# Block sums of feed-forward weights on GpSimd a group ahead, and token sums in place

## The chip, the cores and the metric

The kernel runs on one core of one Trainium2 chip. The metric is the device time of one execution in microseconds, lower is better: the median of several runs. TensorE does the matrix products, VectorE (DVE) and ScalarE (ACT) and GpSimd (POOL) the elementwise work, and SyncE (SP) issues the DMAs.

## The reference, cut to what matters

The reference is a two-layer decoder in float32: 512 tokens, width 1024, 16 heads, feed-forward width 2816. Layer 0 mixes tokens by stick-breaking attention, layer 1 by dilated attention. Each layer then does

```python
def _swiglu(h, w_gate, w_up, w_down):
    return (jax.nn.silu(h @ w_gate) * (h @ w_up)) @ w_down

h = h + _swiglu(_rmsnorm(h, norm_ffn[layer]), w_gate[layer], w_up[layer], w_down[layer])
```

The change touches only the two products `h @ w_gate` and `h @ w_up` of both layers.

## The kernel before, in words

Activations lie transposed: 1024 channels are 8 chunks of 128 partitions, with the 512 tokens along the free axis. A float32 product is made of three matmuls: every weight tile and every activation is split into a high part (fp32r, written by ACT, L306) and the remainder (a DVE subtraction, L307), and high x high, high x low and low x high are added in PSUM.

**The feed-forward.** The 2816 hidden channels are 22 chunks f of 128. Chunks 0 and 1 are computed plainly (`first_tiles`). Chunks 2 to 21 go in ten groups g of two chunks. For each chunk the gate and the up weights and the two halves of the channels form a 2x2 matrix of blocks, w00, w01 (gate) and w10, w11 (up), each 128x512; the tokens are halved too, and seven products P1 to P7 take the place of eight (a Strassen-Winograd scheme). Three products use raw blocks. Four use sums of blocks: S1 = w10 + w11, S2 = S1 + w00, S3 = w10 + w00, S4 = S2 + w01. The order in a group is P1, P2, P6 (S2), P5 (S1), P7 (S3), P4, P3 (S4), for both chunks each, 24 matmuls of 256 columns per product. Beside the products run the down projections (`down`) of earlier chunks, up to eight in a group, as `ffn_order` and `BESIDE` list them.

**Weights.** The class `Weights` is a stream. `load` has SP fetch blocks in their order of first use into two rings of eight slots (raw, raw2); a slot is free after the last product that uses its block. `split` makes one product's operand: where it is a sum, DVE adds first (L280, L281 for S1 and S2, into tiles called sum; L287 for S3, in place; L291 for S4, in place in the tile of S2), then ACT writes the high part and DVE the low part. `get` hands an operand to TensorE and calls `split` up to six operands ahead, as far as the rings allow. The 160 sums (20 chunks, four sums, two layers) are all DVE's before the change.

**Token sums.** Four of the seven products also need sums of token blocks. `token_sums` copies the normalised activations into B (128 x 8 x 512), makes four sums of 128x1024 on DVE (L919, L923, L927, L931) into two tiles tk, and splits each into XT (L913, L916). `first_tiles` lays these steps beside the matmuls of chunk 1.

**Elementwise work of a group.** After P2 DVE adds and scales the gate; after P7, P4 and P3 it adds the up parts (L1016, L1018, L1025). GpSimd multiplies each up tile by the row of scale factors (`scaled_up`, L968), and DVE multiplies gate and up (L971). GpSimd has little else to do here: L866 in `first_tiles`, which multiplies the gate of chunks 0 and 1, and later the gains of layer 1's weights (L305).

**Order.** Each engine works through its own queue in order. The framework inserts the semaphores and may place independent instructions of an engine otherwise than the source does: in the trace the four small column steps (L467 to L470) alternate with the token sums.

Of the kernel before, what the change touches and what calls it, by code (L numbers as in the profile page):

```python
# [7 lines left out]
F = mybir.dt.float32  # L8
# [71 lines left out]
def weight_stream():  # L80


    units, ops, place = [], [], {}

    def unit(key, width):
        if key not in place:
            place[key] = len(units)
            units.append((key, width))
        return place[key]

    for layer in range(2):
        for kind, i in mixer_order():
            r = (kind, layer, i)
            for j in range(4):
                gain = None
                if layer == 1 and kind == "qk":
                    which, part = (j % 2, j // 2) if crossed(r) else (j // 2, j % 2)
                    gain = ("k", (G_MIX1, G_KV)[which] + 4 * part)
                elif layer == 1 and kind == "v":
                    gain = ("v", G_KV + 2 * j)  # L100
                ops.append((kind, "mix", ("raw", unit((*r, j), 512)), gain))
        for step in ffn_order():
            if step[0] == "gu":
                for j in range(4):
                    ops.append(("gu", "mix", ("raw", unit(("gu", layer, step[1], j), 512)), None))
            elif step[0] == "dn":
                a, b = PARTS[step[1]]
                held = layer == 1 and step[1] == len(PARTS) - 1
                ops.append(("dn", "held" if held else "ffn",
                            ("raw", unit(("dn", layer, *step[1:]), 128 * (b - a))), None))  # L110
            else:
                for i in range(2):
                    f = 2 * step[1] + i
                    w = lambda r, c: unit(("w", layer, f, r, c), 512)
                    what = {"P1": lambda: ("raw", w(0, 0)), "P2": lambda: ("raw", w(0, 1)),
                            "P6": lambda: ("s2", w(1, 0), w(1, 1), w(0, 0)), "P5": lambda: ("s1",),
                            "P7": lambda: ("s3", w(1, 0), w(0, 0)), "P4": lambda: ("raw", w(1, 1)),
                            "P3": lambda: ("s4", w(0, 1))}[step[2]]()
                    ops.append(("pr", "ffn", (*what, i) if what[0][0] == "s" else what, None))
    return units, ops  # L120


# [67 lines left out]
class Weights:  # L190
# [8 lines left out]
    def __init__(self, tc, pool, wflat, gains):  # L199
        self.tc, self.nc, self.pool, self.w, self.gains = tc, tc.nc, pool, wflat, gains  # L200
        self.units, self.ops = weight_stream()
        self.offs = np.concatenate([[0], np.cumsum([128 * n for _, n in self.units])]).tolist()
        last = {}
        for n, op in enumerate(self.ops):
            for u in self.used(op):
                last[u] = n
        self.ends = {}
        for u, n in last.items():
            self.ends.setdefault(n, []).append(u)
        first = {}  # L210
# [18 lines left out]
        self.pools = {"raw": pool, "w": pool}  # L229
        self.rt, self.wt, self.sums = {}, {}, {}  # L230
        self.nload = self.nsplit = self.nget = 0

    @staticmethod
    def used(op):
        what = op[2]
        return {"raw": what[1:], "s2": what[1:4], "s1": (), "s3": what[1:3], "s4": what[1:2]}[what[0]]

    def load(self):
        u = self.nload
# [28 lines left out]
    def split(self):  # L268
# [6 lines left out]
        r = [self.rt[v] for v in self.used(self.ops[u])]  # L275
        if what[0] == "raw":
            v = r[0]
        elif what[0] == "s2":
            s1, s2 = (self.pools["sum"].tile([128, 512], F, name="sum", bufs=4) for _ in range(2))
            nc.vector.tensor_add(s1, r[0], r[1])  # L280
            nc.vector.tensor_add(s2, s1, r[2])  # L281
            self.sums[what[-1]] = (s1, s2)
            v = s2
        elif what[0] == "s1":
            v = self.sums[what[-1]][0]
        elif what[0] == "s3":
            nc.vector.tensor_add(r[0], r[0], r[1])  # L287
            v = r[0]
        else:
            v = self.sums.pop(what[-1])[1]  # L290
            nc.vector.tensor_add(v, v, r[0])  # L291
        n = v.shape[1]
        ring = self.oring[u]
        if ring == "held":
# [17 lines left out]
            self.live[self.uring[v]] -= 1  # L312
        self.nsplit += 1
        self.loads()

    def get(self, kind):
        u = self.nget
# [11 lines left out]
def trunk(ctx, tc, xg, wflat, cst_d, cs_d, outT):  # L329
# [510 lines left out]
    def ffn(layer, done):  # L840
# [36 lines left out]
        def first_tiles(p, XT):  # L877
# [3 lines left out]
            both("gu", banks)  # L881
            sums, columns, rows = rstd_steps(pjbank)
            sums()
            tau1, tau2, low1, low2, tau4, tau3, low4, low3 = token_sums(p, XT)
# [15 lines left out]

        def token_sums(p, XT):

            B = p.tile([128, 8, 512], F, name="B")
            t = [p.tile([128, 4, 256], F, name=f"tk{i}") for i in range(2)]
            b12, b21, b22 = B[:, 0:4, 256:512], B[:, 4:8, 0:256], B[:, 4:8, 256:512]
            b11 = B[:, 0:4, 0:256]

            def block(c):
                g = gains[:, (G_FFN0, G_FFN1)[layer] + c:(G_FFN0, G_FFN1)[layer] + c + 1]
                act.activation(B[:, c, :], H[:, c, :], AF.Copy, scale=g)  # L910

            def high(i, v):
                act.activation(XT[:, i, 0], v, AF.Copy)  # L913

            def low(i, v):
                dve.tensor_sub(XT[:, i, 1], v, XT[:, i, 0].bitcast(F))  # L916

            def first():
                dve.tensor_sub(t[0], b11, b12)  # L919
                high(1, t[0])  # L920

            def second():
                dve.scalar_tensor_tensor(t[1], t[0], -1.0, b22, op0=OP.mult, op1=OP.subtract)  # L923
                high(0, t[1])
# [11 lines left out]
            return [first, second, lambda: low(1, t[0]), lambda: low(0, t[1]), fourth, third,  # L936
                    lambda: low(3, t[0]), lambda: low(2, t[1])]

        st = {}

# [40 lines left out]
        def product(g, p, XT):  # L981
# [16 lines left out]
                    stepped()  # L998
            a, b, c, e = (st.get(k) for k in "abce")
            f0 = 2 * g  # L1000
            if p == "P1":
                st["g", 0] = TS()
                act.activation(st["g", 0], a, AF.Copy)
            elif p == "P2":
# [95 lines left out]
        order = ffn_order()  # L1100
        with tc.tile_pool(name=f"ff{layer}", bufs=1, reuse_waits="tile") as fp:
            XT = fp.tile([128, 4, 2, 4, 256], FR, name="XT")
            W.pools["w2"] = fp
            with tc.tile_pool(name=f"tk{layer}", bufs=1, reuse_waits="tile") as tp:
                first_tiles(tp, XT)
            with tc.tile_pool(name=f"wr{layer}", bufs=1, reuse_waits="tile") as wp:
                W.pools["raw2"] = W.pools["sum"] = wp
                W.loads()
                for step in order[2:]:
                    if step[0] == "pr":  # L1110
                        product(*step[1:], XT)
# [51 lines left out]
```

## Time and profile before

| what | value |
|---|---|
| median of 3 runs | 1210.62 us (1208.28 to 1211.24) |
| profiled execution: its own time, its span | 1206.98 us, 1205.1 us |
| mean granted TensorE clock | 0.997 |
| PE busy | 1185.0 us, 98% |
| DVE busy | 1011.8 us, 84% |
| ACT busy | 698.5 us, 58% |
| POOL busy | 173.8 us, 14% |
| DVE, low parts of weights (L307, four largest groups) | 206.8 + 71.0 + 45.6 + 37.4 us |
| DVE, block sums (L280, L281, L287, L291) | 160 instructions, mean 686 to 740 ns |
| POOL, `scaled_up` (L968) | 40 instructions, mean 1563 ns |

Busy is the time in which an engine executes an instruction; an instruction that is held up by something that the profile doesn't name counts as busy for longer. The matmuls are pipelined, so a busy PE is not a PE at its peak. The feed-forward of layer 0 with its sums runs from about 254 us to 610 us of the span, that of layer 1 from about 846 us to the end.

### The profile page before, as it was taken

The numbers are of one execution on the slowest core, as the hardware profiler recorded it, in microseconds if no ns is written. First come the engines' busy times: TensorE is split into PE (matmuls) and PEld (weight loads), VectorE is DVE, ScalarE is ACT, GpSimd is POOL, SyncE is SP. The second block draws the span as 40 slices with busy tenths as digits, with TensorE's granted clock in tenths as the row PEclk, the third lists the DMA queues.
The fourth block names the chain that finished last, engine by engine and source line by source line (L and its number), as shares of the span: only waits on it lengthen the run. The fifth ranks groups of instructions, "written<-read, shape, count | busy, mean of one in ns | idle before, by whom it ended". The sixth has DMA issues, their size and how long they took to land.

```text
span 1205.1 us, 21100 instructions
## 1 busy us (share of the span) xinstructions
PE 1185.0 (98%) x7501; PEld 1059.8 (88%) x7501; DVE 1011.8 (84%) x1831; ACT 698.5 (58%) x1331; POOL 173.8 (14%) x237
## 2 busy tenths in 40 slices
PE   9999999999999999999999999999999999999997
PEld 7989888888999999999788889887789999999996
DVE  6799999899987878787868899788899878787865
ACT  6667676685544444454466677767755444445443
POOL 0000000001100000014235443110111000000111
PEclk9999999999999999999999999999999999999998
DMA  7654644234243323332154656551343333333112
GB/s 265 177 147 113 159 114 124 62 105 140 88 125 95 115 88 114 98 106 88 36 142 132 158 136 178 133 149 53 96 141 124 113 100 102 98 113 89 45 61 70
DMA packets 74360, 138.30 MB, mean 115 GB/s; under 512 B 9616, under 2 KB 13712, under 8 KB 74256
## 3 DMA queue, kind: packets, MB, share of 16 engines
q1 hardware_dynamic: 74256, 136.97, 40.0%
q8 instruction: 59, 0.97, 0.3%
q14 instruction: 45, 0.37, 0.1%
HBM read 106.00 MB, written 2.10 MB: 90 GB/s over the span
## 4 chain that ended last, share of the span: by engine, by line
PE 87%; DVE 6%; issue 2%; DMA 2%; ACT 2%; SPq 1%; POOL 1%; POOLq 0%; DVEq 0%
PE pj L387 39%; PE z L387 30%; PE t L387 12%; PE av L387 3%; PE t L703 3%; DVE wlo L307 1%; DMA mov<-hl 1%; DMA raw<-wflat 1%; DVE w2lo L307 0%; DVE H L751 0%; SPq L243 0%; DMA H<-xg 0%; POOL H L1076 0%; DMA rp<-rp 0%; DVE sum L281 0%
## 5 line engine op out<-in xcount | busy, mean ns | idle before, releaser
L306 ACT ACTIVATE whi<-raw 128x512 fp32r<-128x512 f32 (+1 forms) x290 | 178.7, 622 | 134.5 <-PE pj L387 52.1
L307 DVE TENSOR_TENSOR wlo<-raw,whi 128x512 fp32r<-128x512 f32 (+1 forms) x290 | 206.8, 721 | 26.0 <-ACT whi L306 23.6
L387 PE MATMUL pj<-VO,whi 128*128 128x512 f32 x568 | 180.7, 398 | 1.1 <-DVE H L751 1.0
L387 PE MATMUL pj<-X,whi 128*128 128x512 f32 x480 | 154.4, 402 | 0.4
L968 POOL TENSOR_TENSOR up<-up,R 128x512 f32<-128x512 f32 x40 | 62.4, 1563 | 490.9 <-DVE up L1016 442.6
L387 PEld LDWEIGHTS pj<-VO,whi 128*128 128x128 f32 x568 | 102.4, 189 | 23.8 <-ACT whi L306 1.1
L387 PE MATMUL pj<-VO,wlo 128*128 128x512 f32 x284 | 112.7, 397 | 0.0
L751 DVE TENSOR_TENSOR H<-H,pj 128x512 f32<-128x512 f32 (+1 forms) x120 | 79.3, 664 | 32.2 <-PE pj L387 31.5
L387 PEld LDWEIGHTS pj<-X,whi 128*128 128x128 f32 x480 | 86.9, 188 | 19.1 <-ACT X L423 0.9
L387 PE MATMUL z<-XT,whi 128*128 128x256 f32 x560 | 99.7, 280 | 0.0
L306 ACT ACTIVATE w2hi<-raw 128x512 fp32r<-128x512 f32 (+1 forms) x102 | 62.8, 617 | 59.0 <-PE z L387 17.1
L387 PE MATMUL z<-X,whi 128*128 128x256 f32 (+1 forms) x464 | 96.1, 301 | 0.0
L387 PE MATMUL pj<-X,wlo 128*128 128x512 f32 x240 | 95.2, 396 | 0.5 <-DVE wlo L307 0.5
L387 PEld LDWEIGHTS z<-XT,whi 128*128 128x128 f32 x560 | 86.2, 189 | 0.7
L387 PE MATMUL pj<-VO,w2hi 128*128 128x512 f32 x264 | 83.1, 396 | 0.4 <-ACT VO L974 0.4
L307 DVE TENSOR_TENSOR w2lo<-raw,w2hi 128x512 fp32r<-128x512 f32 (+1 forms) x102 | 71.0, 698 | 12.0 <-ACT w2hi L306 11.7
L387 PEld LDWEIGHTS z<-X,whi 128*128 128x128 f32 x464 | 74.9, 189 | 4.7
L387 PE MATMUL z<-XT,wlo 128*128 128x256 f32 x280 | 78.5, 280 | 0.0
L387 PE MATMUL pj<-whi,X 128*128 128x256 f32 x384 | 74.9, 285 | 2.1 <-DVE rp L558 2.1
L387 PE MATMUL z<-XT,w2hi 128*128 128x256 f32 x400 | 74.0, 284 | 1.7 <-ACT w2hi L306 1.0
L305 POOL TENSOR_TENSOR raw<-raw,H 128x512 f32<-128x512 f32 x48 | 58.9, 1237 | 79.0 <-DMA raw<-wflat 37.1
L387 PE MATMUL z<-X,wlo 128*128 128x256 f32 (+1 forms) x232 | 69.8, 301 | 0.0
(200 smaller groups left out, 3033.0 us busy)
## 6 DMA issues: line engine op xcount, KB each, us to landing
raw<-wflat SPq DMA_DIRECT2D x384, 256.0 KB, 2.8
mov<-hl SPq DMA_DIRECT2D x64, 256.0 KB, 4.3
sta<-hl SPq DMA_DIRECT2D x64, 128.0 KB, 2.3
rp<-rp SPq DMA_DIRECT2D x56, 64.0 KB, 2.1
raw<-wflat SPq DMA_DIRECT2D x16, 128.0 KB, 2.6
H<-xg SPq DMA_DIRECT2D x7, 256.0 KB, 5.5
outT<-H SPq DMA_DIRECT2D x2, 512.0 KB, 3.0
CS<-cs SPq DMA_DIRECT2D x1, 512.0 KB, 3.7
```

Source lines behind the costliest of these rows:

```text
L305: nc.gpsimd.tensor_mul(v3, v3, g.unsqueeze(2).to_broadcast([128, n // m, m]))
L306: nc.scalar.activation(hi[:, :n], v, AF.Copy)
L307: nc.vector.tensor_sub(lo[:, :n], v, hi[:, :n].bitcast(F))
L387: pe.matmul(out, a, b, start=start, stop=stop, skip_group_check=True)
L703: pe.transpose(b[:, o:o + 128], pr[i][:, 128 * c:128 * c + 128], idf)
L751: dve.tensor_add(H[:, n, e], H[:, n, e], p[:, e])
L968: pool.tensor_mul(two(u), two(u), r)
```

## The change

GpSimd makes the block sums, called for before their product comes up; `add_ahead` puts a request on a list, and `add_pending`, called after every split, issues it as soon as all blocks of the chunk have been requested from memory and, for a sum written over a block, the product that uses that raw block has been split. A sum not issued by then is made when its operand is split. S1 is written over w10, S2 into a tile sum (one per chunk instead of two), S3 = S2 - w11 over w00, S4 over w01. Requests: in P6 of a group S2 of the next group's two chunks, after P4 and P3 their S3 and at P3 their S4. For the first group S2 of chunk 3 and of chunk 2 are requested in `first_tiles`, chunk 2 by DVE (two additions per layer stay there), S3 when the raw2 ring opens, S4 in P1. The block w10 is last used by P5 instead of P7.

The token sums are made in place in B, now laid out as two token halves; the tiles tk are gone. The first two stay on DVE, the last two (L927 and L931 before) go to GpSimd, and their splits follow later: their high parts and low parts are the last steps beside chunk 1. The tiles sum live in the pool of the whole feed-forward instead of the pool that opens after `first_tiles`.

```diff
+    def add(self, kind, key, eng=None):
+        if (kind, key) in self.sums:
+            return self.sums[kind, key]
+        eng = eng or self.nc.gpsimd
+        u10, u11, u00 = self.blocks[key]["s2"]
+        if kind in ("s1", "s2"):
+            r = [self.rt[u] for u in (u10, u11, u00)]
+            s2 = self.pools["sum"].tile([128, 512], F, name="sum", bufs=4)
+            eng.tensor_add(r[0], r[0], r[1])
+            eng.tensor_add(s2, r[0], r[2])
+            self.sums["s1", key], self.sums["s2", key] = r[0], s2
+        elif kind == "s3":
+            r = self.rt[u00]
+            eng.tensor_sub(r, self.add("s2", key), self.rt[u11])
+            self.sums[kind, key] = r
+        else:
+            r = self.rt[self.blocks[key]["s4"][0]]
+            eng.tensor_add(r, self.add("s2", key), r)
+            self.sums[kind, key] = r
+        return self.sums[kind, key]
+    def add_pending(self):
+        while self.pending:
+            kind, key, eng = self.pending[0]
+            b = self.blocks[key]
+            replaced = {"s2": (), "s3": b["s2"][2:], "s4": b["s4"]}[kind]
+            if (kind, key) not in self.sums and not (
+                    all(u < self.nload for u in b["s2"] + b["s4"])
+                    and all(self.first[u] < self.nsplit for u in replaced)):
+                return
+            self.add(kind, key, eng)
+            self.pending.pop(0)
...
-            nc.vector.tensor_add(s1, r[0], r[1])
-            nc.vector.tensor_add(s2, s1, r[2])
...
-            nc.vector.tensor_add(r[0], r[0], r[1])
...
-            nc.vector.tensor_add(v, v, r[0])
+            v = self.add(*what[:2])
...
-            beside = [(tau1, tau2), (columns, low1, rows, gate), (low2, tau4, times_up, tau3),
-                      (low, low4, low3)]
+            adds = lambda f: lambda: W.add_ahead("s2", (layer, f), dve if f == 2 else None)
+            beside = [(tau1, tau3), (columns, low1, rows, tau2, gate, tau4), (low2, times_up, adds(3), adds(2)),
+                      (low, highs, low34)]
...
             def third():
-                dve.tensor_sub(t[1], b22, b12)
-                high(2, t[1])
+                pool.tensor_sub(b12, b22, b12)
             def fourth():
-                dve.tensor_add(t[0], b21, t[1])
-                high(3, t[0])
+                pool.tensor_add(b21, b21, b11)
...
             elif p == "P6":
+                for key in ahead:
+                    W.add_ahead("s2", key)
...
                 scaled_up()
+                W.add_ahead("s3", ahead[0])
...
                 scaled_up()
+                W.add_ahead("s3", ahead[1])
+                for key in ahead:
+                    W.add_ahead("s4", key)
```

## Rows read from the trace of the kernel before

**Rows 1.** The chain that ended last: shares of the span by engine.

```profile
PE 87%; DVE 6%; issue 2%; DMA 2%; ACT 2%; SPq 1%; POOL 1%; POOLq 0%; DVEq 0%
```

**Rows 2.** Windows: stretch, length, PE, PEld, DVE, ACT, POOL busy (instructions), clock, DMA.

```profile
254.00:334.00 80.00, 77.75 (x535) 71.20 (x533) 77.39 (x121) 46.78 (x79) 9.58 (x6) 1.00 0.38 117
846.00:931.00 85.00, 82.41 (x557) 75.09 (x558) 80.47 (x131) 50.65 (x86) 10.93 (x6) 1.00 0.38 121
...
395.00:426.00 31.00, 31.00 (x206) 28.27 (x205) 25.83 (x42) 14.06 (x25) 2.90 (x2) 1.00 0.41 118
```

**Rows 3.** Waits of PE from 254 to 334 us: total, times, longest.

```profile
PE pj L387 <- DVE H L751: 0.7, 1, 0.7
PE t L387 <- DVE wlo L307: 0.7, 1, 0.7
PE z L387 <- ACT s L1003: 0.6, 1, 0.6
```

**Rows 4.** Waits of PE from 846 to 931 us, the two longest.

```profile
PE z L387 <- DVE w2lo L307: 1.1, 1, 1.1
PE z L387 <- ACT w2hi L306: 1.0, 1, 1.0
```

**Rows 5.** Groups of DVE's block sums, 254 to 334 us: count, busy, mean ns.

```profile
L281 DVE TENSOR_TENSOR sum<-sum,raw 128x512 f32<-128x512 f32 x6 | 5.1, 850 | 0.1
...
L280 DVE TENSOR_TENSOR sum<-raw 128x512 f32<-128x512 f32 x4 | 3.9, 963 | 0.3 <-DMA raw<-wflat 0.3
...
L291 DVE TENSOR_TENSOR sum<-sum,raw 128x512 f32<-128x512 f32 x5 | 3.3, 685 | 0.0
...
L287 DVE TENSOR_TENSOR raw<-raw 128x512 f32<-128x512 f32 x4 | 2.7, 684 | 0.0
...
L280 DVE TENSOR_TENSOR sum<-raw,raw 128x512 f32<-128x512 f32 x2 | 1.4, 683 | 0.0
...
L287 DVE TENSOR_TENSOR raw<-raw,raw 128x512 f32<-128x512 f32 x2 | 1.4, 680 | 0.0
```

**Rows 6.** Timeline of DVE: start, length in us, instruction; two pairs of neighbours.

```profile
263.49 1.22 DVE L927 TENSOR_TENSOR tk<-B 128x1024 f32<-128x1024 f32 x1
264.62 0.15 DVE L469 TENSOR_TENSOR nrm<-nrm 128x4 f32<-128x4 f32 x1
...
317.10 0.68 DVE L307 TENSOR_TENSOR wlo<-raw,whi 128x512 fp32r<-128x512 f32 x1
317.71 0.68 DVE L280 TENSOR_TENSOR sum<-raw,raw 128x512 f32<-128x512 f32 x1
```

**Rows 7.** GpSimd instructions of two lines: shortest, median, longest in ns.

```profile
L968 POOL TENSOR_TENSOR up<-up,R x40: 1287/1612/2827, 288.7 to 1157.4; 128x512 f32<-128x512 f32 x40
...
L1076 POOL TENSOR_TENSOR H<-H,R x7: 725/739/754, 1189.1 to 1200.1; 128x256 f32<-128x256 f32 x7
```

**Rows 8.** Timeline of POOL near 270 us, two instructions back to back.

```profile
270.36 3.06 POOL L866 TENSOR_TENSOR s<-s,R 128x512 f32<-128x512 f32 x2 [32.62 <-ACT s L865]
```

**Rows 9.** Timeline of DVE: instructions beside one of POOL, and one 256-wide alone.

```profile
270.59 1.66 DVE L281 TENSOR_TENSOR sum<-sum,raw 128x512 f32<-128x512 f32 x1
272.18 1.78 DVE L280 TENSOR_TENSOR sum<-raw 128x512 f32<-128x512 f32 x1
...
287.49 0.42 DVE L307 TENSOR_TENSOR wlo<-raw,whi 128x256 fp32r<-128x256 f32 x1
...
321.33 1.77 DVE L307 TENSOR_TENSOR w2lo<-raw,w2hi 128x512 fp32r<-128x512 f32 x1
...
886.31 1.20 DVE L307 TENSOR_TENSOR wlo<-raw,whi 128x256 fp32r<-128x256 f32 x1
...
919.99 1.20 DVE L307 TENSOR_TENSOR w2lo<-sum,w2hi 128x512 fp32r<-128x512 f32 x1
```

**Rows 10.** Waits of SP's queue, 254 to 290 us: total, times, longest.

```profile
SPq L243 <- DVE tk L927: 4.4, 1, 4.4
```

**Rows 11.** Waits of DVE in the whole span: total, times, longest.

```profile
DVE s L971 <- POOL up L968: 22.8, 18, 2.2
```

More of the change, by code (lines that the diff above doesn't have):

```diff
@@ L114, in weight_stream @@
                     w = lambda r, c: unit(("w", layer, f, r, c), 512)
+                    b = (layer, f)
                     what = {"P1": lambda: ("raw", w(0, 0)), "P2": lambda: ("raw", w(0, 1)),
[L116 to L119, printed above, removed]
+                            "P6": lambda: ("s2", b, w(1, 0), w(1, 1), w(0, 0)), "P5": lambda: ("s1", b, w(1, 0)),
+                            "P7": lambda: ("s3", b, w(0, 0), w(1, 1)), "P4": lambda: ("raw", w(1, 1)),
+                            "P3": lambda: ("s4", b, w(0, 1))}[step[2]]()
+                    ops.append(("pr", "ffn", what, None))
     return units, ops
@@ L229, in __init__ @@
         self.pools = {"raw": pool, "w": pool}
+        self.blocks = {op[2][1]: {} for op in self.ops if op[2][0] == "s2"}
+        for op in self.ops:
+            if op[2][0] in ("s2", "s4"):
+                self.blocks[op[2][1]][op[2][0]] = op[2][2:]
+        self.first, self.pending = first, []
         self.rt, self.wt, self.sums = {}, {}, {}
@@ L235, in used, with add_ahead @@
         what = op[2]
-        return {"raw": what[1:], "s2": what[1:4], "s1": (), "s3": what[1:3], "s4": what[1:2]}[what[0]]
+        return what[1 if what[0] == "raw" else 2:]
+    def add(self, kind, key, eng=None):
[18 more added lines that the diff above has]
+        return self.sums[kind, key]
+    def add_ahead(self, kind, key, eng=None):
+        if key in self.blocks:
+            self.pending.append((kind, key, eng))
+            self.add_pending()
+    def add_pending(self):
[9 more added lines that the diff above has]
+            self.pending.pop(0)
     def load(self):
@@ L277, in split @@
             v = r[0]
-        elif what[0] == "s2":
-            s1, s2 = (self.pools["sum"].tile([128, 512], F, name="sum", bufs=4) for _ in range(2))
-            nc.vector.tensor_add(s1, r[0], r[1])
-            nc.vector.tensor_add(s2, s1, r[2])
[L282 to L286, printed above, removed]
-            nc.vector.tensor_add(r[0], r[0], r[1])
-            v = r[0]
-        else:
-            v = self.sums.pop(what[-1])[1]
-            nc.vector.tensor_add(v, v, r[0])
+        else:
+            v = self.add(*what[:2])
         n = v.shape[1]
@@ L314, in split @@
         self.loads()
+        self.add_pending()
     def get(self, kind):
@@ L883, in first_tiles @@
             sums()
-            tau1, tau2, low1, low2, tau4, tau3, low4, low3 = token_sums(p, XT)
+            tau1, low1, tau2, low2, tau3, tau4, highs, low34 = token_sums(p, XT)
             gate, times_up, low = hidden(0, banks)
-            beside = [(tau1, tau2), (columns, low1, rows, gate), (low2, tau4, times_up, tau3),
-                      (low, low4, low3)]
+            adds = lambda f: lambda: W.add_ahead("s2", (layer, f), dve if f == 2 else None)
+            beside = [(tau1, tau3), (columns, low1, rows, tau2, gate, tau4), (low2, times_up, adds(3), adds(2)),
+                      (low, highs, low34)]
             banks = [zbank(), zbank()]
@@ L901, in token_sums @@
         def token_sums(p, XT):
[L903 to L906, printed above, removed]
+            B = p.tile([128, 2, 8, 256], F, name="B")
+            b11, b12, b21, b22 = B[:, 0, 0:4], B[:, 1, 0:4], B[:, 0, 4:8], B[:, 1, 4:8]
             def block(c):
                 g = gains[:, (G_FFN0, G_FFN1)[layer] + c:(G_FFN0, G_FFN1)[layer] + c + 1]
-                act.activation(B[:, c, :], H[:, c, :], AF.Copy, scale=g)
+                act.activation(B[:, :, c, :], H[:, c, :].rearrange("p (e n) -> p e n", e=2), AF.Copy, scale=g)
             def high(i, v):
@@ L918, in first, with highs @@
             def first():
-                dve.tensor_sub(t[0], b11, b12)
-                high(1, t[0])
+                dve.tensor_sub(b11, b11, b12)
+                high(1, b11)
             def second():
-                dve.scalar_tensor_tensor(t[1], t[0], -1.0, b22, op0=OP.mult, op1=OP.subtract)
-                high(0, t[1])
+                dve.scalar_tensor_tensor(b11, b11, -1.0, b22, op0=OP.mult, op1=OP.subtract)
+                high(0, b11)
             def third():
-                dve.tensor_sub(t[1], b22, b12)
-                high(2, t[1])
+                pool.tensor_sub(b12, b22, b12)
             def fourth():
-                dve.tensor_add(t[0], b21, t[1])
-                high(3, t[0])
+                pool.tensor_add(b21, b21, b11)
+            def highs():
+                high(2, b12)
+                high(3, b21)
             for c in range(8):
                 block(c)
-            return [first, second, lambda: low(1, t[0]), lambda: low(0, t[1]), fourth, third,
-                    lambda: low(3, t[0]), lambda: low(2, t[1])]
+            return [first, lambda: low(1, b11), second, lambda: low(0, b11), third, fourth, highs,
+                    lambda: (low(2, b12), low(3, b21))]
         st = {}
@@ L1000, in product @@
             f0 = 2 * g
+            ahead = [(layer, f) for f in (f0 + 2, f0 + 3)]
             if p == "P1":
+                if g == 1:
+                    for f in (f0, f0 + 1):
+                        W.add_ahead("s4", (layer, f))
                 st["g", 0] = TS()
@@ L1102, in ffn @@
             XT = fp.tile([128, 4, 2, 4, 256], FR, name="XT")
-            W.pools["w2"] = fp
+            W.pools["w2"] = W.pools["sum"] = fp
             with tc.tile_pool(name=f"tk{layer}", bufs=1, reuse_waits="tile") as tp:
@@ L1106, in ffn @@
             with tc.tile_pool(name=f"wr{layer}", bufs=1, reuse_waits="tile") as wp:
-                W.pools["raw2"] = W.pools["sum"] = wp
+                W.pools["raw2"] = wp
                 W.loads()
+                for f in (2, 3):
+                    W.add_ahead("s3", (layer, f))
                 for step in order[2:]:
```

## The prediction

> **What bounds the kernel now.** I read the chain of waits first: TensorE holds 87% of it, DVE 6% [rows 1]. So a change to DVE and GpSimd counts only where TensorE waits for them. The windows say where that is. In a middle group of the feed-forward TensorE is busy 31.00 of 31.00 us and DVE 25.83 [rows 2]: DVE has 5 us to spare and nothing is to be won. In the stretch from the token sums to the end of group 2 it differs: DVE is busy 77.39 of 80 us in layer 0 and 80.47 of 85 in layer 1, and TensorE lacks 80 - 77.75 = 2.25 and 85 - 82.41 = 2.59 us, 4.84 together [rows 2]. The waits agree: low parts, high parts and residuals that came late, 0.3 to 1.1 us each [rows 3, 4]. These two stretches are what can be won, 4.84 us at most, 0.4% of the span.
>
> **What the change takes from DVE there.** In the first stretch DVE makes 6 + 4 + 5 + 4 + 2 + 2 = 23 block sums [rows 5]: eight each of groups 1 and 2 and seven of group 3. Two (S1 and S2 of chunk 2) stay, 21 go. One lasts 0.68 us, but the next instruction starts 0.61 us after it [rows 6], so 21 x 0.61 = 12.8 us. Of the four token sums two go; the next instruction starts 264.62 - 263.49 = 1.13 us after one [rows 6], so 2.3 us. Together 15.1 us per stretch. The splits of these two sums stay and come later; they are the same 4 instructions and count as nothing.
>
> **What it adds on GpSimd.** No row shows a plain addition of 128x512 on GpSimd; the product of the same shape takes 1.29 us at the least, 1.61 in the median [rows 7]. I take 1.29 as the price undisturbed. For 128x1024 the step from 256 to 512 columns (0.74 to 1.29, rows 7) gives 1.29 + 2 x 0.55 = 2.4 us, an estimate; nothing under 1.29 and nothing over 2 x 1.61 would fit these rows. In the stretch that is 21 x 1.29 + 2 x 2.4 = 31.9 us beside the 9.58 it has [rows 2]: 52% of 80 us, so GpSimd can carry it, and across a middle group 8 x 1.29 beside 2.90, 13.2 of 31 us.
>
> **What that does to DVE.** This is the term that decides. When GpSimd ran two products back to back from 270.36 on [rows 8], the two DVE sums beside them took 1.66 and 1.78 us instead of 0.69; others took 1.77, 1.20 (a 256-wide one that takes 0.42 alone) and 1.20 [rows 9]. So a DVE instruction that reads two SBUF tensors is held while GpSimd reads its own, and each GpSimd instruction costs DVE something. How much? In layer 0's stretch GpSimd has 6 instructions [rows 2], and five DVE instructions beside them (the first and the last of layer 0 stand in rows 9) are longer by 4.4 us; in layer 1's, 6 and three (first and last there too) by 1.8. That is 6.2 / 12 = 0.52 us each. The ends: 0.30, the mean of layer 1 alone (1.8 / 6), and 1.09, the longest (1.78 - 0.69). The twelve follow an addition out of PSUM or an ACT result, so some meet DVE at work that isn't held; the sums come at any time. I take 0.65, nearer to the mean than to the longest, and 0.65 x 2.4 / 1.29 = 1.2 for a token sum. Then 21 x 0.65 + 2 x 1.2 = 16.1 us against 15.1 taken away: DVE gains nothing, it has 1.0 us more to do per stretch. The two balance at 0.61 us per sum.
>
> The Trainium skill states a stricter rule (SBUF — State Buffer, Who interferes with whom): the pair of ports that DVE and GpSimd share is an exclusive lock, and an instruction with two SBUF inputs waits for a GpSimd one that reads SBUF to its end. The 1.78 us of rows 9 agrees with it, the mean of 0.52 only if half the meetings miss; its time is that of the second rival below.
>
> **What of it reaches TensorE.** DVE has 80 - 77.39 = 2.6 and 85 - 80.47 = 4.5 us idle in the stretches [rows 2] and operands are split up to six ahead, though the waits show that this lead is used up here. I let half of the 1.0 through: 0.5 per layer, 1.0 us. Against it stands layer 1's wait for a high part that waits for a sum, 1.0 us [rows 4]: that is S2 of chunk 3, which GpSimd now makes beside DVE's S2 of chunk 2. The others stay, since what is late in them is DVE's queue as a whole; the 0.6 us of rows 3 is ACT's. Sum: 1206.98 + 1.0 - 1.0 = 1207.0 us for the profiled execution. The median of the runs is 3.64 us above it (1210.62 - 1206.98), so 1210.6.
>
> **Middle groups.** DVE loses 8 x 0.61 = 4.9 us and is held for 8 x 0.65 = 5.2: 26.1 of 31 us instead of 25.83. TensorE stays covered. I cost these at nothing; the cover is the 5 us of idle time.
>
> **Queues and DMAs that move.** GpSimd's adds wait for their blocks' DMAs and, where they write over a block, for the DVE low part made from it; behind them in the queue stand the scaling of `scaled_up` and then DVE's L971, which already waits for GpSimd 18 times, 22.8 us in all [rows 11], without TensorE idling in the middle groups. SP's loads into the raw2 ring lie in memory over B: one of them waited 4.4 us for the last token sum that reads B [rows 10]. Now B is read until its last low parts, later beside chunk 1, and that wait grows by some us. The raw2 blocks are those of the first down projections, whose products come after group 1's P7; I cost it at nothing; if that lead is too short, at no more than the 4.4 us of this row. S1 over w10 frees its slot at P5 instead of P7: nothing waits for more.
>
> **The rivals.**
> *First: the sums were what made DVE late.* A sum no longer stands between a block and its high part, so operands are ready early though DVE is as full as before. For it: both waits of rows 4 are in the P6 products, on S2. Against it: rows 3 name a residual and a raw block's low part, which come behind the queue. At best all 4.84 us go: 1202.1 profiled, 1205.8 in the median.
> *Second: the held port costs the full price.* Each sum holds DVE for 1.0 us (rows 9: 0.97 and 1.09 back to back). Then 21 x 1.0 + 2 x 1.85 = 24.7 - 15.1 = 9.6 us more per stretch, less DVE's idle 2.6 and 4.5: 7.0 + 5.1 = 12.1 us, 1219.1 profiled, 1222.7. It decides from 0.83 us per sum, where the two stretches lose 3.6 us beyond their idle time. For it: DVE is full in these stretches, so an instruction is always there to be held. Against it: the twelve instructions of the same stretches averaged 0.52.
> With 1.09 and 2.0 for the token sums it is 22.9 + 4.0 - 15.1 = 11.8, less 2.6 and 4.5: 16.5 us, 1227.1 in the median, the upper end of the unknown cost; with 0.30 the loss is below zero by more than the 4.84 us that there are to win, the lower end, 1205.8.
> *Third: GpSimd's queue.* L971 waits behind the sums in every middle group. The groups have 31 - 26.1 = 4.9 us of DVE idle; two scalings, each late by two held sums (1.29 + 0.65 = 1.9 each), are 7.6, so 2.7 us too much in each of about 12 full groups: 32 us, 1243. It decides from 2.45 us per scaling. Against it: a scaling comes several products after the S2 requests.
> *Fourth: not ahead.* The 16 slots hold 12 blocks of a group and little of the next, so S2 is issued late, on an engine that needs 2.6 us for it instead of 1.2. Six operands of lead hide it in the middle groups; in the second group of each layer, where there is no lead, its two chunks cost 2 x (1.4 + 0.65) = 4.1 us: 8 us for both layers, 1218.8.
>
> **How the numbers follow.** Forecast 0.45 (its own range 1207 to 1214), first rival 0.22, second 0.20, third 0.08, fourth 0.05. A measurement here can tell about 0.3%, 3.6 us, from no change. Faster is the first rival: 0.22. Same is the forecast: 0.45. Slower are the rest: 0.33. The range goes from 1205, just under the lower end, to 1226, which takes in the second and the fourth rival and leaves out the third and the far end of the second.
>
> **What would show it.** Right: DVE busy in the two stretches within 3 us of 77 and 80 although it has 21 sums fewer, low parts of 1.2 to 1.8 us scattered through all groups, GpSimd near 174 + 156 x 1.45 + 4 x 2.4 = 410 us busy, TensorE still 31.00 of 31.00 in the middle groups, and its wait for the high part in layer 1 gone. Wrong: DVE well under 75 us busy in the first stretch (the port costs less and the first rival holds), TensorE idle over 4 us in a stretch (the second), DVE waiting for L968 over 60 us in all and TensorE idle in the middle groups (the third), or TensorE waiting at P6 for a high part that waits for GpSimd (the fourth).

## The result, and the profile after

The changed kernel takes 1255.41 us in the median of 4 runs (1254.02 to 1256.43), the kernel before 1210.76 beside it: ratio 1.0372, 95% interval 1.0354 to 1.0390. It is 44.65 us slower. The profiled execution took 1254.02 us, its span is 1252.2 us (before 1205.1) and the mean granted clock 0.986.

The busy times of the engines, from the page of the changed kernel:

```profile
PE 1198.3 (96%) x7501; PEld 1070.4 (85%) x7501; DVE 1022.5 (82%) x1671; ACT 692.6 (55%) x1331; POOL 419.3 (33%) x397
```

TensorE executes the same 7501 matmuls, is busy 1198.3 - 1185.0 = 13.3 us longer and idle 53.9 - 20.1 = 33.8 us longer; that is the span's 47.1. DVE has 160 instructions fewer (1671 against 1831) and is busier by 10.7 us.

Where TensorE idles, by stage: start and middle groups of layer 0, then the same of layer 1. The columns are those of [rows 2].

```profile
254.00:337.00 83.00, 72.26 (x459) 65.21 (x458) 70.39 (x86) 40.55 (x68) 47.47 (x29) 0.94 0.35 102
337.00:600.00 263.00, 253.55 (x1741) 234.52 (x1741) 206.59 (x265) 118.79 (x206) 120.45 (x82) 0.99 0.33 97
848.00:935.00 87.00, 77.97 (x408) 66.11 (x407) 75.89 (x99) 50.66 (x88) 37.23 (x23) 0.94 0.31 94
935.00:1165.00 230.00, 219.66 (x1549) 205.16 (x1548) 182.59 (x232) 104.32 (x181) 104.89 (x71) 0.99 0.32 96
```

It lacks 10.74, 9.45, 9.03 and 10.34 us in them; before, the two starts lacked 2.25 and 2.59 and a middle group nothing [rows 2]. In the middle groups DVE is busy 206.59 of 263 us and GpSimd 120.45, so no engine beside TensorE is full where TensorE waits. That points to a chain of waits, not to a full engine.

**The chain in the middle groups.** It shows in the idle times in front of three instructions. In the groups of lines (count | busy, mean ns | idle before it and who ended it), the scaling, the product behind it, the gate's scaling and the largest group of low parts in the changed kernel:

```profile
L1005 POOL TENSOR_TENSOR up<-up,R 128x512 f32<-128x512 f32 x40 | 61.6, 1542 | 35.2 <-DVE up L1060 32.0 <-DVE up L1062 1.9 <-DMA raw<-wflat 1.3
L1008 DVE TENSOR_TENSOR s<-s,up 128x512 f32<-128x512 f32 x40 | 39.1, 979 | 42.9 <-POOL up L1005 36.5 <-ACT s L1000 4.2 <-ACT nrm L1002 1.2
L997 DVE TENSOR_TENSOR s<-s,R 128x512 f32<-128x512 f32 x20 | 22.4, 1120 | 0.0
L342 DVE TENSOR_TENSOR wlo<-raw,whi 128x512 fp32r<-128x512 f32 x334 | 277.4, 843 | 42.6 <-ACT whi L341 41.7 <-PE av L423 0.2
```

and two of these in the kernel before:

```profile
L307 DVE TENSOR_TENSOR wlo<-raw,whi 128x512 fp32r<-128x512 f32 x280 | 201.4, 726 | 26.0 <-ACT whi L306 23.6 <-PE z L387 1.2 <-PE av L387 0.2
L968 POOL TENSOR_TENSOR up<-up,R 128x512 f32<-128x512 f32 x40 | 62.4, 1563 | 490.9 <-DVE up L1016 442.6 <-DVE up L1018 48.3
```

Before, GpSimd stood idle 490.9 us ahead of the 40 scalings, and in 35 of the 40 places it was waiting for the up tile. After it is 35.2 us and 9 places; in nearly all the others GpSimd comes to the scaling straight from other work. And DVE's elementwise instructions, at 0.69 us alone, last 0.98 (L1008) and 1.12 us (L997).

One such place in order of time, near 400 us of the changed kernel. First GpSimd:

```profile
396.36 1.76 POOL L1005 TENSOR_TENSOR up<-up,R 128x512 f32<-128x512 f32 x1
398.07 1.74 POOL L259 TENSOR_TENSOR raw<-sum,raw 128x512 f32<-128x512 f32 x1
399.78 1.29 POOL L263 TENSOR_TENSOR raw<-sum,raw 128x512 f32<-128x512 f32 x1
401.03 1.29 POOL L1005 TENSOR_TENSOR up<-up,R 128x512 f32<-128x512 f32 x1
```

then, of the same stretch, DVE, ACT and TensorE:

```profile
396.88 0.68 DVE L1062 TENSOR_TENSOR up<-up,t 128x512 f32<-128x512 f32 x1
...
402.36 1.76 DVE L1008 TENSOR_TENSOR s<-s,up 128x512 f32<-128x512 f32 x1 [3.69 <-POOL up L1005]
...
404.15 0.63 ACT L1011 ACTIVATE VO<-s 128x512 fp32r<-128x512 f32 x1 [5.65 <-DVE s L1008]
...
407.35 0.63 ACT L1000 ACTIVATE s<-s 128x512 f32<-128x512 f32 x1 [2.04 <-DVE s L997]
...
409.96 0.58 ACT L1045 ACTIVATE s<-z 128x512 f32<-128x512 f32 x1
...
410.59 0.51 PE L423 MATMUL z<-XT,w2hi 128*128 128x256 f32 x2 [2.75 <-ACT s L1045]
```

The up tile is ready at 397.56 (396.88 + 0.68). Its scaling starts at 401.03, 3.47 us late, behind an S3 and an S4. DVE's product L1008 waits 3.69 us and is then held by the next S4 (1.76 us instead of 0.69). ACT waits 5.65 us for it. Behind ACT's instruction stands, in its own queue, the rest of ACT's work: L1000, which waits another 2.04 us for a DVE that is late by now, and at last L1045, which copies the gate of P1 out of its PSUM bank. P6 writes into that bank, so TensorE waits 2.75 us. Four links, none of them on a full engine. It happens in every second middle group: eight stalls of 1.9 to 2.8 us. The waits of the changed kernel over the whole span (us in total, times, longest) give the size of three of the links:

```profile
POOL raw L254 <- DMA raw<-wflat: 145.5, 16, 11.8
...
DVE s L1008 <- POOL up L1005: 36.5, 20, 3.7
...
PE z L423 <- ACT s L1045: 20.6, 10, 2.8
```

**The starts.** TensorE's waits in the two start stretches of the changed kernel (us in total, times, longest), layer 0 and layer 1:

```profile
PE t L423 <- DVE wlo L342: 4.2, 1, 4.2
PE pj L423 <- DVE H L787: 2.7, 1, 2.7
PE pj L511 <- DVE rtok L506: 1.7, 1, 1.7
...
PE pj L511 <- DVE rtok L506: 4.0, 1, 4.0
PE pj L423 <- DVE H L787: 3.1, 1, 3.1
```

They stand in place of waits of 0.6 to 1.1 us [rows 3, 4]. Three of their causes, in the timelines of GpSimd and DVE in layer 0:

```profile
260.87 2.79 POOL L965 TENSOR_TENSOR B<-B 128x1024 f32<-128x1024 f32 x1 [2.42 <-DVE B L958]
...
276.49 1.73 POOL L263 TENSOR_TENSOR raw<-sum,raw 128x512 f32<-128x512 f32 x1
278.18 2.48 POOL L902 TENSOR_TENSOR s<-s,R 128x512 f32<-128x512 f32 x2
```

```profile
261.72 2.50 DVE L254 TENSOR_TENSOR raw<-raw 128x512 f32<-128x512 f32 x1
...
279.47 0.69 DVE L905 TENSOR_TENSOR s<-s,z 128x512 f32<-128x512 f32 x1 [2.39 <-POOL s L902]
...
281.31 0.68 DVE L342 TENSOR_TENSOR wlo<-raw,whi 128x512 fp32r<-128x512 f32 x1
...
304.31 1.74 DVE L1008 TENSOR_TENSOR s<-s,up 128x512 f32<-128x512 f32 x1 [1.17 <-POOL up L1005]
305.98 0.68 DVE L787 TENSOR_TENSOR H<-H,pj 128x512 f32<-128x512 f32 x1
```

A sum of DVE beside a token sum on GpSimd takes 2.50 us instead of 0.69, and behind it in DVE's queue are the steps to rtok. The gate scaling L902 starts behind S3, S3 and S4; DVE's L905 waits 2.39 us for it, and the low part that TensorE needs stands behind L905. The waits for the residual (H, L787: 2.7 and 3.1 us) are the up scaling once more: L1008 waits 1.17 us for it and is then held for 1.74, and the residual stands behind L1008 in DVE's queue.

**The clock.** After some of these stalls the granted clock of TensorE fell to half, its level of 1.2 GHz. Windows of the changed kernel after the stall of 2.7 us (304.0 to 306.7) and at the stall of 4.2 us (277.85 to 282.04):

```profile
307.20:310.40 3.20, 3.20 (x12) 2.72 (x11) 3.20 (x5) 0.67 (x2) 3.20 (x3) 0.50 0.00 0
...
279.90:286.50 6.60, 4.46 (x21) 4.46 (x22) 6.06 (x9) 3.20 (x6) 2.45 (x2) 0.50 0.06 12
```

In all the clock stood at 0.50 for 27.2 us ahead of the tail: one stretch of 6.8 us and six of 3.4 us (read off such windows over the whole span). TensorE was busy in 24.2 us of them and still waiting in 3.0, so half the rate costs 12.1 us of matmul time, most of the 13.3 by which its busy time grew. So about a quarter of the loss is not waiting but slower matmuls after a wait.

### The profile page after: what moved, and what is told of

Same layout as the page of the kernel before. It is cut to its first block, busy times and chain, and to the rows that moved or that the text cites. A ratio compares the mean times of both kernels' runs of the same rounds, so it can differ in the third digit from the quotient of the medians.

```text
span 1252.2 us, 21163 instructions
## 1 busy us (share of the span) xinstructions
PE 1198.3 (96%) x7501; PEld 1070.4 (85%) x7501; DVE 1022.5 (82%) x1671; ACT 692.6 (55%) x1331; POOL 419.3 (33%) x397
## 5 line engine op out<-in xcount | busy, mean ns | idle before, releaser
L342 DVE TENSOR_TENSOR wlo<-raw,whi 128x512 fp32r<-128x512 f32 (+1 forms) x344 | 283.4, 836 | 45.7 <-ACT whi L341 44.8
L341 ACT ACTIVATE whi<-raw 128x512 fp32r<-128x512 f32 (+1 forms) x344 | 210.7, 621 | 145.6 <-PE pj L423 56.7
L342 DVE TENSOR_TENSOR w2lo<-raw,w2hi 128x512 fp32r<-128x512 f32 (+1 forms) x128 | 115.7, 911 | 20.8 <-ACT w2hi L341 20.5
L341 ACT ACTIVATE w2hi<-raw 128x512 fp32r<-128x512 f32 (+1 forms) x128 | 78.4, 618 | 78.6 <-PE z L423 27.0
L787 DVE TENSOR_TENSOR H<-H,pj 128x512 f32<-128x512 f32 (+1 forms) x120 | 79.3, 664 | 26.2 <-PE pj L423 25.5
L423 PE MATMUL z<-XT,w2hi 128*128 128x256 f32 x400 | 77.4, 293 | 12.4 <-ACT s L1045 12.4
L423 PEld LDWEIGHTS z<-XT,w2hi 128*128 128x128 f32 x400 | 65.9, 201 | 14.3 <-ACT s L1045 13.6
L1011 ACT ACTIVATE VO<-s 128x512 fp32r<-128x512 f32 x40 | 25.2, 629 | 91.7 <-DVE s L1008 91.7
```

The source lines that it names most:

```text
L341: nc.scalar.activation(hi[:, :n], v, AF.Copy)
L342: nc.vector.tensor_sub(lo[:, :n], v, hi[:, :n].bitcast(F))
L423: pe.matmul(out, a, b, start=start, stop=stop, skip_group_check=True)
L787: dve.tensor_add(H[:, n, e], H[:, n, e], p[:, e])
L1011: act.activation(hi, two(g), AF.Copy)
```

## The experiments

Three theories. **Q**, GpSimd's queue: scalings stand behind sums, and the chain above follows. **P**, the held port: a DVE instruction with two SBUF operands is held while GpSimd reads its own, and DVE's work is late. **R**, the requests: sums ahead and in place order and block things otherwise, whoever makes them. All ratios are to runs of the kernel before on the same chip.

**The scaling of the up half to DVE.**

```diff
 def scaled_up():
-    pool.tensor_mul(two(u), two(u), r)
+    dve.tensor_mul(two(u), two(u), r)
```

> The changed kernel with the scaling of the up tiles (40 instructions) on DVE in place of GpSimd; the block sums stay on GpSimd. Theory Q (GpSimd's queue: the scaling stands behind sums, DVE waits for it, ACT waits for DVE, TensorE for ACT): the 19.8 us that TensorE idles in the middle groups, 9.45 us from 337 to 600 and 10.34 from 935 to 1165, fall below 4, and the time to 1225 to 1237; the two starts keep their loss. Theory P (the held port alone): DVE has 40 instructions more and is held as before, so 1255 or more.

Measured 1236.36 us (1234.63 to 1238.99), ratio 1.0222 [1.0203, 1.0241]. 19.05 us come back. Windows of the middle groups, layer 0 and 1:

```profile
337.00:600.00 263.00, 262.03 (x1791) 241.88 (x1790) 230.78 (x294) 125.41 (x214) 96.27 (x66) 1.00 0.33 97
...
935.00:1165.00 230.00, 228.43 (x1599) 213.56 (x1600) 198.08 (x252) 109.86 (x188) 89.33 (x59) 0.99 0.35 102
```

DVE is 24 us busier there than after the change and TensorE idles 0.97 us instead of 9.45, in layer 1 1.57 instead of 10.34. A fuller DVE, and less waiting: in the middle groups it was the chain. At the starts TensorE still lacks 12.7 and 10.0 us: the waits for the residual fell from 5.8 to 0.9 us, but those for L1045 grew to 5.1 and 4.5.

**Sums of 8 columns.** Every block sum is cut to 8 of its 512 columns, so the other columns aren't summed; requests and order stay, and the sums S2 go round four fixed tiles in place of the pool's. The token sums stay whole and on GpSimd.

```diff
-            eng.tensor_add(r[0], r[0], r[1])
+            c = slice(0, 8)
+            eng.tensor_add(r[0][:, c], r[0][:, c], r[1][:, c])
...
```

> The changed kernel with each block sum cut to 8 of its 512 columns (the other columns are left out, so the sums are not made); every instruction, its order and its waits stay. Q and P both: neither queue nor port costs anything, so all but the token sums' share is gone and DVE has 100 us less to do: 1203 to 1213. Theory R (the requests ahead, the writing over blocks and the new waits of the loads cost the time, not the length of the sums): 1235 or more.

Measured 1210.53 us, ratio 1.0002 [0.9993, 1.0011]. R falls: with the requests and waits of the change and hardly any work in them nothing is lost. It says more: DVE is busy 920.9 us, 91 less than before, and the kernel isn't faster. Taking the block sums off DVE wins nothing here, though the token sums on GpSimd may hide a gain: with them come two waits at rtok that the kernel before hasn't (first line, of TensorE's waits; the second is of DVE's timeline),

```profile
PE pj L513 <- DVE rtok L508: 3.4, 2, 1.8
...
261.92 1.98 DVE L256 TENSOR_TENSOR raw<-raw 128x8 f32<-128x8 f32 x1
```

and no run made short block sums with the token sums on DVE. The second line shows the hold by itself: DVE's sum of 8 columns, 0.13 us in layer 1, takes 1.98 beside a token sum of GpSimd and ends at 263.90, with that one's end at 263.87.

**A busy queue without reads.** As above, and GpSimd fills the time with two memsets for each sum, which write only.

```diff
+    def filler(self, eng, t):
+        if eng is self.nc.gpsimd:
+            eng.memset(t[:, 8:512], 0.25)
+            eng.memset(t[:, 8:512], 0.5)
```

> As the run before, but behind each short sum GpSimd fills the rest of the tile twice with a constant, which writes SBUF and reads nothing: about the time of a full sum in the queue without its reads (the sums are not made). Q: as slow as the changed kernel, 1240 to 1256, with low parts on DVE back near 0.69 us. P: 1205 to 1216.

Measured 1212.48 us, ratio 1.0025 [1.0014, 1.0035]. Low parts and the product in this kernel's groups of lines, and the memsets ahead of a scaling in GpSimd's timeline:

```profile
L353 DVE TENSOR_TENSOR wlo<-raw,whi 128x512 fp32r<-128x512 f32 x334 | 240.7, 727 | 62.6 <-ACT whi L352 60.0 <-DMA raw<-wflat 1.3
L1019 DVE TENSOR_TENSOR s<-s,up 128x512 f32<-128x512 f32 x40 | 28.5, 712 | 36.9 <-POOL up L1016 30.5 <-ACT s L1011 4.2 <-ACT nrm L1013 1.2
```

```profile
384.46 0.20 POOL L268 TENSOR_TENSOR raw<-sum,raw 128x8 f32<-128x8 f32 x1
384.60 0.52 POOL L275 MEMSET raw<- 128x504 f32 x1
385.18 0.52 POOL L276 MEMSET raw<- 128x504 f32 x1
385.67 1.29 POOL L1016 TENSOR_TENSOR up<-up,R 128x512 f32<-128x512 f32 x1
```

GpSimd is busy 375.3 us and low parts still take 0.727 us, as before and not 0.843. The product waits 30.5 us for the scaling over the span, against 36.5 after the change and 22.8 before [rows 11], and in the middle groups TensorE lacks 0.27 us. So Q alone fails for a queue of this length: the memsets ahead of the scalings cost 2 us over the kernel (1212.48 - 1210.53) as long as no instruction is held. (The memsets don't always stand right behind their sum, and a filled sum takes 1.2 us, not 1.5, so the queue is shorter than the real one: the longest wait for a scaling is 2.5 us, against 3.7. A queue as long as the real one without held instructions wasn't run.)

**All block sums to DVE**, ahead and in place as changed, token sums still on GpSimd.

```diff
-        eng = eng or self.nc.gpsimd
+        eng = eng or self.nc.vector
```

> The changed kernel with all block sums on DVE, still requested a group ahead and written over their blocks; the two token sums stay on GpSimd. Q and P: the loss of the block sums goes, 1208 to 1216, near the kernel before. R: 1235 or more.

Measured 1212.58 us, ratio 1.0022 [1.0012, 1.0032]. So the loss, but for 2 us, is the engine and not the order.

**Only the block sums on GpSimd.** Both scalings and both token sums go to DVE.

```diff
-                pool.tensor_mul(two(u), two(u), r)
+                dve.tensor_mul(two(u), two(u), r)
-                pool.tensor_mul(t, t, R)
+                dve.tensor_mul(t, t, R)
-                pool.tensor_sub(b12, b22, b12)
+                dve.tensor_sub(b12, b22, b12)
-                pool.tensor_add(b21, b21, b11)
+                dve.tensor_add(b21, b21, b11)
```

> The changed kernel with everything of GpSimd but the block sums given to VectorE: the scaling of the up half, the scaling of the first tiles' gate half and both token sums. Left beside a busy GpSimd are VectorE's held instructions alone. Scaling alone on VectorE measured 1236.4 us (e1_scale_dve), with stalls of TensorE left in the two start stretches of 1.9, 4.2, 1.1, 5.1 and 4.2, 1.6, 0.7, 4.5 us. Theory 'gate and tokens' (the starts are lost because the gate scaling stands behind three sums on GpSimd and because the token sums hold the column sums): the 4.2 and the 1.9 go in both layers, and the slow clock behind them: 1216 to 1224 us. Theory 'held VectorE' (the starts are lost because VectorE, which has more work there than elsewhere, has its sums stretched to 1.7 us): the stalls move but stay, 1228 to 1240 us.

Measured 1229.60 us, ratio 1.0168 [1.0151, 1.0186]. The theory 'held VectorE' holds at the starts, though 6.8 us went with the gate scaling and the token sums together: the stall of 4.2 us before wlo in layer 0 gave way to two of 0.8 and 1.8, that at rtok in layer 1 fell from 4.0 to 1.7, and that at rtok in layer 0 stayed (1.75 and 1.55). What is left can be seen in the timelines of DVE, ACT and TensorE in this kernel, where nothing on DVE or TensorE waits for a scaling of GpSimd:

```profile
311.73 1.78 DVE L997 TENSOR_TENSOR s<-s,R 128x512 f32<-128x512 f32 x1
...
315.13 1.75 DVE L1008 TENSOR_TENSOR s<-s,up 128x512 f32<-128x512 f32 x1
```

```profile
313.54 0.63 ACT L1000 ACTIVATE s<-s 128x512 f32<-128x512 f32 x1 [6.05 <-DVE s L997]
...
318.48 0.57 ACT L1045 ACTIVATE s<-z 128x512 f32<-128x512 f32 x1
...
319.11 0.79 PE L423 MATMUL z<-XT,w2hi 128*128 128x256 f32 x2 [5.03 <-ACT s L1045]
```

GpSimd has sums back to back from 301.3 to 316.3 us, DVE is busy without a gap and from 302 to 317 us each of its instructions with two SBUF operands lasts 1.2 to 1.8 us. ACT waits 6.05 us for L997, and TensorE waits 5.03 us for L1045: the same end of the chain as in the middle groups, reached by lateness alone.

**Sums on GpSimd from chunk 6 on** ("column block" below is a chunk f of the hidden channels), those of the chunks before and the token sums on DVE; then the same with the up scaling on DVE.

```diff
-        eng = eng or self.nc.gpsimd
+        eng = eng or (self.nc.gpsimd if key[1] >= 6 else self.nc.vector)
```

> The changed kernel with the sums of column blocks 0 to 5 of either layer and both token sums on VectorE, and GpSimd's block sums only from column block 6 on, that is for the middle groups, with the scaling of the up half on GpSimd as in the changed kernel. Theory 'joined' (the middle groups lose by themselves, since the scaling stands behind stretched sums): the start stretches are as in e4_sums_on_dve, the stalls of about 2 us in every second group stay, 1226 to 1236 us. Theory 'carried over' (the middle groups only pay for VectorE being late from the start): 1209 to 1216 us.

> As e6_late_sums, but with the scaling of the up half on VectorE: GpSimd holds VectorE in the middle groups and nothing waits for its queue but the low parts of its sums. Theory 'joined': with no start loss and no scaling behind the sums nothing is left, 1209 to 1214 us. Theory 'held VectorE' (the held time itself is the loss, about 0.7 us for each of some 104 sums, wherever they run): 1225 us or more.

Measured 1243.31 us, ratio 1.0278 [1.0258, 1.0299], and 1218.60 us, ratio 1.0068 [1.0053, 1.0082]. The first is 'joined' and worse than expected: the middle groups lose by themselves, 30.2 us over the kernel with all sums on DVE (next): by the two profiled executions 22.4 us of idle TensorE and 7.8 us of longer matmuls. It is not carried over from the start. Their window in layer 0, and TensorE's wait in it:

```profile
337.00:600.00 263.00, 253.29 (x1706) 233.53 (x1706) 204.74 (x262) 118.06 (x205) 118.54 (x81) 0.99 0.32 97
```

```profile
PE z L423 <- ACT s L1045: 10.8, 4, 2.8
```

and the same window with the scaling on DVE:

```profile
337.00:600.00 263.00, 262.40 (x1754) 240.53 (x1753) 229.82 (x291) 125.27 (x213) 100.81 (x68) 1.00 0.34 98
```

One line of code moves 24.7 us. The second misses both expectations: what it loses over all sums on DVE, 5.5 us, is what GpSimd's sums cost in the middle groups with no scaling behind them, by held instructions and by whatever waits for the sums themselves. 'Joined' had that at nothing.

**Everything on DVE**, requests ahead and in place (block sums and token sums); then without asking ahead, each sum at its split.

```diff
 def add_ahead(self, kind, key, eng=None):
-    if key in self.blocks:
+    if False:
```

> The changed kernel with all block sums and both token sums on VectorE: only the asking ahead and the sums in place are left of the change. e4_sums_on_dve (token sums still on GpSimd) measured 1212.6 us with two stalls of about 1.9 us at the wait for the rows of the norm that a held column sum explains. If that reading holds, these two stalls go: 1207 to 1211 us, the same as before or just under it. If asking ahead itself costs the 2 us: 1212 to 1214 us.

> As e8_all_on_dve (block sums and token sums on VectorE, both in place), but no sum is asked for ahead: each is made where its product's weights are split, as in the kernel before. Left of the change are the sums in place alone. e8_all_on_dve measured 1213.1 us against 1210.6 before. Theory 'ahead costs the 2.5 us' (block sums on VectorE before the columns and low parts that the start waits for): 1209 to 1211.5 us. Theory 'in place costs it' (the token sums in place set a high part, a low part and the next sum one behind the other, and e8_all_on_dve still has a stall of 2.5 us in layer 1 before the first product with wlo): 1212 to 1214.5 us.

Measured 1213.10 us (12 runs), ratio 1.0021 [1.0010, 1.0031], and 1210.99 us (12 runs), ratio 1.0001 [0.9991, 1.0012]. Giving the token sums to DVE won nothing: the stalls of about 1.9 us at rtok are gone as read, others came in their place. Asking ahead costs about 2.1 us (the intervals overlap a little, so it is hardly clear of noise), in place nothing that can be told. Waits of TensorE at layer 1's start, ahead and not ahead:

```profile
PE t L423 <- DVE wlo L342: 2.6, 2, 2.4
```

```profile
PE t L423 <- DVE wlo L342: 1.0, 1, 1.0
```

The reading is that a sum made earlier on DVE stands ahead of a low part that is needed sooner.

**Half of the sums on GpSimd**, all else on DVE: S1 and S2 first, then S3 and S4.

```diff
-        eng = eng or self.nc.gpsimd
+        eng = self.nc.gpsimd if kind in ("s1", "s2") and eng is None else self.nc.vector
```

> As e5_only_block_sums (1229.6 us: only the block sums on GpSimd, scaling, gate scaling and token sums on VectorE), but S3 and S4 are made by VectorE too, so that GpSimd makes S1 and S2 alone, half of the sums. With none on GpSimd it is 1213.1 us (e8_all_on_dve). Theory 'linear' (each sum of GpSimd costs its share of held time): about 1221 us, 1218 to 1224. Theory 'threshold' (VectorE has slack, and is late only where several held instructions stand in a row before a product's end): at most 1216 us. A third reading, that the loss comes from S1 and S2 because the low parts of the streams wait for GpSimd to make them: 1226 us or more.

> The counterpart of e10_half_the_sums: GpSimd makes S3 and S4, VectorE makes S1 and S2 and all else. S1 and S2 alone on GpSimd measured 1214.9 us, all four 1229.6, none 1213.1. Theory 'threshold' (neither half is dear by itself, and the loss comes when both stand in one stretch): 1213 to 1218 us. Theory 'S3 and S4' (the dear half is the one whose low parts VectorE takes last, close to the product that needs them): 1224 to 1230 us.

Measured 1214.90 us, ratio 1.0035 [1.0018, 1.0052], and 1218.30 us, ratio 1.0062 [1.0038, 1.0086], just over the upper end of its expectation. Over all on DVE that is 1.8 us, which is within the noise, and 5.2 us, together 7.0; all four kinds on GpSimd cost 16.5 (1229.60 - 1213.10). So the loss grows faster than the number of sums. That short lateness is taken up by the lead of the operands and long rows of sums are not is the likely reason, but no run shows it by itself. 'Threshold' is right for S1 and S2, and nearly for S3 and S4.

**The 44.65 us, in steps of these kernels:** in place +0.4 (not clear of noise), ahead +2.1, the sums of the middle groups on GpSimd +30.2, the sums of chunks 2 to 5 and the token sums on GpSimd the remaining 12.1 (1255.41 - 1243.31). Or by mechanism, on top of the first two: block sums beside DVE with no scaling behind them +16.5, the gate scaling and the token sums on GpSimd +6.8 (1236.36 - 1229.60), the up scaling behind the sums +19.0. The size of a step depends on the order in which the steps are taken: the same line for the scaling is worth 19.0 us here and 24.7 with the sums from chunk 6 on. No version was faster than the kernel before. What no run took apart is how the 12.1 us of the starts divide between the three causes shown in the timelines and the held DVE.

## Why the prediction was wrong

**The step that failed** is "Middle groups. DVE loses 8 x 0.61 = 4.9 us and is held for 8 x 0.65 = 5.2: 26.1 of 31 us instead of 25.83. TensorE stays covered. I cost these at nothing; the cover is the 5 us of idle time." The sum for DVE was good, DVE does keep its idle time (206.59 of 263). But idle time summed over a group covers only what may be done at any time in it. The product L1008 may not: it stands between a scaling on GpSimd and a high part on ACT, and ACT's queue carries the copy that frees TensorE's bank. A delay of 3.5 us and a held instruction went down this chain in every second group and came out as 1.9 to 2.8 us of waiting; with the clock and the stalls in the groups just before, that is 30.2 us. The third rival had this mechanism, and its 1243 us is what the middle groups alone make of it (1243.31). It was given 0.08; against it stood "a scaling comes several products after the S2 requests". That is the order of the source; in the trace the requests are drawn out, since S1 waits for its blocks (145.5 us for DMAs in 16 places), and S3 and S4, not S2, stand right ahead of the scaling. Its own sum was by DVE's idle time again and its mark, DVE waiting over 60 us for the scaling, wasn't reached (36.5 us): waiting was long enough at less, because it goes on through ACT. So that the numbers agree is chance.

**The held port** was mis-sized a little. Before, DVE was busy 1011.8 us; without 156 block sums at 0.69 and 4 token sums at 1.2 [rows 6, 9] it would be 899.4. It is 1022.5, so by this estimate 160 instructions of GpSimd held it for 123 us, 0.77 each against the 0.65 taken, with ends of 0.30 and 1.09. That is above the balance of 0.61 by 0.16, about 3.4 us for 21 sums. The 1.78 us [rows 9] was no exception: 1.75 to 1.78 stands again and again in the rows above.

The Trainium skill (SBUF — State Buffer, Who interferes with whom) says that a DVE instruction with two SBUF inputs contends with a GpSimd one that reads SBUF and not with one that only writes it. The memset run agrees: 0.727 us beside memsets, 0.843 beside sums.

**What the sum left out.** First, GpSimd is held as well: 1.29 us was the price undisturbed, and its sums lasted 1.45 to 1.61 in the mean by group, so that rows of them are longer; the mark for GpSimd's busy time had reckoned with that (410 us, measured 419.3), the middle groups' sum had not. Second, the clock: 13.3 us of longer matmuls that stood in no term. Third, the starts: "I let half of the 1.0 through" stood against 12.1 us measured. The second rival had the place and 12.1 us too, by a price of the hold of 1.0 us, against 0.77 measured; the causes read in the timelines were the queue at L902, the token sum beside DVE's S1, the scaling ahead of the residual and L997 held in a row of sums, so the agreement of the numbers is partly chance. Its sign came true, TensorE idle over 4 us in a stretch. Another mark misled: DVE was busy 70.39 and 75.89 us in the starts, not within 3 us of 77 and 80 and in the first under the 75 that was to mean a cheaper port. The port wasn't cheaper; DVE stood waiting itself, 2.39 us for L902 alone.

**What held.** That DVE gains nothing, since the hold eats what the sums leave; that layer 1's wait for a high part goes; that raw2's loads behind B cost nothing that TensorE sees; that little was to be won: with DVE relieved of 91 us the time is the same, and even without the 3.4 us of waits that the token sums brought there the gain would stay within the 4.84. The first rival, with 4.84 us won in the changed kernel, is refuted by the 44.65 lost. So is the fourth: TensorE doesn't wait once for a high part of the w2 ring in the changed kernel.

## What to carry to other kernels

An idle share covers work that can be done at any time; a link in a chain across engines is covered only by the slack of that chain. So before work is put on an idle engine, follow what this engine already does for others: here GpSimd's idle 490.9 us ahead of 40 short scalings was not spare time but the reason why they were hardly ever late. And measure the ceiling first: cutting the sums to 8 columns shows in one run how little there was to win by taking them from DVE.

## What the runs showed of the hardware

- The hold works both ways. Beside GpSimd's sums, DVE's 128x512 instructions with two SBUF operands take 1.2 to 1.8 us instead of 0.69, and GpSimd's up to 1.76 in the stretch shown near 400 us, where the two that met an idle DVE (399.78 and 401.03) took 1.29. A DVE instruction with one operand in PSUM isn't lengthened: L1062 took 0.68 us beside a scaling, and the 20 of L1060 all took 0.67 to 0.69.
- GpSimd's memset of 128x504 float32 takes 0.52 us and leaves DVE's instructions at their length (low parts 0.727 us).
- The granted clock fell to half for 3.4 or 6.8 us around seven of the stalls, either while TensorE still waited (at 279.8 in the stall from 277.85 to 282.04) or up to 1.5 us after it resumed (307.1 after 306.7, 904.4 after 902.9). The length of a stall alone didn't decide: that of 2.8 us at 407.8 was followed by none, that of 1.8 us at 901.1 was. One stretch of 3.4 us at half rate costs up to 1.7 us, about as much as the shortest of these stalls.
